# Elementwise work of the mixers moved from GpSimd to DVE and ScalarE in a hybrid decoder block

## The chip, the cores and the metric

The kernel runs on one core of a Trainium2 chip. TensorE (PE) multiplies matrices into PSUM; DVE (VectorE), ScalarE (ACT) and GpSimd (POOL) do elementwise work; SP and ACT issue the DMAs. Each engine takes its instructions strictly in the order written, and semaphores order them between engines. The metric is the device time of one execution in microseconds; before the change the median of three runs is 1366.57 us (1365.25 to 1368.38).

## The reference

One decoder layer on 1024 tokens of width 1024, float32. A normalised input is projected by one matrix; sixteen heads mix the tokens in three ways; an output projection and a squared-ReLU MLP follow.

```python
proj = rms_norm(x, norm1_g) @ w_in            # split into hq hf hi hg | sq sk sv | fq fk fv ff
# 4 HGRN heads (per head 64 keys, 64 values), in chunks of 64 tokens:
b = cumsum(log_f);  k = (1 - lb) * sigmoid(-f)
A[t,s] = sum_k q[t,k] k[s,k] exp(b[t,k] - b[s,k])          # s <= t, inside a chunk
o = (q * exp(b)) @ S + A @ v;  S = exp(b_end) * S + (k * exp(b_end - b)).T @ v
o_hg = rms_norm(o, hg_norm_g) * silu(hg)
# 6 stick-breaking heads, q and k RMS-normed per head, s < t:
z = q @ k.T / 8;  A = exp(log_sigmoid(z) + sum over later s of log_sigmoid(-z))
# 6 forgetting heads, q and k RMS-normed: softmax(q @ k.T / 8 + c_t - c_s), s <= t
x = x + concat(o_hg, A_sb @ sv, A_fox @ fv) @ w_out
x = x + square(relu(rms_norm(x, norm2_g) @ w_ff1)) @ w_ff2
```

## The kernel before

All large products run as three matmuls on split operands: each float32 matrix is cut into a rounded high part and the rest (`split`, L129: the high part by ScalarE or a chosen engine, the low part by a subtraction), and high x high, high x low and low x high are summed (`mm3`, L173 to L176).

The mixing stage works through eight units in the order of `CFG["ORDER"]`: m0, hg0, m1, m2, m3, hg1, m4, m5. A unit m*i* is a pair of one stick-breaking and one forgetting head ("pair i" below); a unit hg*j* is two HGRN heads. While the core of one unit runs, the projection of the next is computed: `tok` (L289) and `qf`/`ig` (L601, L612) are its matmuls (tile `pj`), `w_steps` (L204) loads its eight weight slices into four raw buffers and splits them (tiles `whi`, `wlo`; the letter of `CFG["LO"]` at the unit's place names the engine of the low part, V for DVE and G for GpSimd). `finish` (L307) squares keys and queries (`qsq`), sums the squares and scales the keys (`kraw`). During the last unit's core the output weights are split (`woh`, `wol`, L820) and the output projection starts (`po`).

The stick-breaking part (`qtile`, L404 to L418) clips the scores, takes exp and log on ScalarE, sums from the right by a DVE scan (`sbr`, L413), subtracts that sum from the scores (`sbz`, L416) and takes exp again. `qprep` (L360) copies and scales the queries on GpSimd (`qd`).

The HGRN core (`hgrn`, L629) replaces the decay inside a chunk by six levels of blocks, 32 down to 1 tokens wide. At each level and for each half of the tokens, DVE subtracts the value of `b` at the block's middle (`hx`, L671), ScalarE takes two exponentials (L673, L674), four products with the queries give `hxq` (L676, per half and head) and two with the keys update `hx` (L677); PE then multiplies (`hz`, L681) and DVE copies the result under a mask (`hat`, L692). The diagonal (`hqk`, L698), the state (`hkd`, L714 to L716, and `hb`, L725) and the output (L742 to L790) follow. The gates of a core, `hg_gates` (L568), are computed before it.

The order of instructions on each engine is not the order of this code. The builder runs its own timeline estimate over the program and places each instruction by it (`TCARGS`, L35), with the order of the timed steps (L906 to L923) and the priority of the weight splits (`HPW`) as its input. A change of engine at one line therefore moves instructions on all engines. Pools of fixed numbers of buffers (`CFG["BUFS"]`: five `zs` buffers hold `hx`, `hkd`, `sbz`) limit how far it can run ahead.

Of the kernel before, what the change touches and what calls it, by code (L numbers as in the profile page):

```python
# [12 lines left out]
AF = mybir.ActivationFunctionType  # L13
ALU = mybir.AluOpType
# [4 lines left out]
P = 128  # L19
# [4 lines left out]
HD = 64  # L24
# [31 lines left out]
    "GT": ["pair", "pair", "pair"],
# [9 lines left out]
def hybrid_block(ctx, tc, x, lb_logits, norm1_g, w_in, hg_norm_g, sb_q_g, sb_k_g, fox_q_g, fox_k_g,  # L66
# [215 lines left out]
    def proj_attn(name, pr):  # L282
# [24 lines left out]
        def finish(half):  # L307
            q8, k8 = (a.rearrange("p t a d -> p (t a) d") for a in (st["q"][half], st["kr"][half]))
            ss = small.tile([P, 16], F32, name="qss")
            for e, a in enumerate((k8, q8)):  # L310
                sq = big("dt", "qsq", [P, 8, HD])
                ENG[CFG["FE"][pr][0]].tensor_tensor(out=sq, in0=a, in1=a, op=ALU.mult)
# [3 lines left out]
            ENG[CFG["FE"][pr][1]].tensor_tensor(out=k8, in0=k8, in1=r[:, 0:8].unsqueeze(2).broadcast_to([P, 8, HD]), op=ALU.mult)

# [37 lines left out]
    def attn(name):  # L355
# [23 lines left out]
        def qtile(h, i):  # L379
# [16 lines left out]
            for c, w in reversed(pcs):  # L396
# [7 lines left out]
                if sbk:  # L404


                    e = big("e", "sbe")[:, :w]
                    zs = big("zs", "sbz")[:, :w]
                    V.tensor_scalar(out=zs, in0=z, scalar1=st["r"][i // 4][:, i % 4, 0:1], scalar2=ZMAX, op0=ALU.mult, op1=ALU.min)  # L409
                    S.activation(e, zs, AF.Exp)  # L410
                    S.activation(e, e, AF.Ln, bias=1.0)  # L411
                    r = big("r", "sbr")[:, :w]
                    V.tensor_tensor_scan(out=r[:, ::-1], data0=e[:, ::-1], data1=zero_t[:, 0:1].broadcast_to([P, w]),  # L413
                                         initial=0.0 if prev is None else prev, op0=ALU.add, op1=ALU.add)
                    prev = r[:, 0:1]
                    ENG[CFG["SUB"][pr]].tensor_tensor(out=zs, in0=zs, in1=r, op=ALU.subtract)  # L416
# [151 lines left out]
    def hg_gates(name, half):  # L568
# [60 lines left out]
    def hgrn(name):  # L629
# [16 lines left out]
        def level(n):  # L646
            def lv(t):
                return t.rearrange("p (b e n) -> p b e n", e=2, n=n)
# [17 lines left out]
            for half in range(2):  # L666
# [8 lines left out]
                for h in range(2):  # L675
                    ENG[CFG["HQ"][pr][h]].tensor_tensor(out=qv(xq, h, half), in0=qv(x_, h, None), in1=qv(q, h, None), op=ALU.mult)  # L676
                ENG[CFG["HK"][pr]].tensor_tensor(out=lv(x_)[:, :, 0, :], in0=lv(x_)[:, :, 0, :], in1=lv(k)[:, :, 0, :], op=ALU.mult)  # L677
            ph = pt("zt"[li % 2], "hz")
# [28 lines left out]
        def state():  # L707
            eb = small.tile([P, NC_], F32, name="heb")
            kt = []
            for half in range(2):  # L710
# [4 lines left out]
                S.activation(kd, kd, AF.Exp)  # L715
                G.tensor_tensor(out=kd, in0=kd, in1=k, op=ALU.mult)  # L716
                S.activation(eb[:, half * HC:(half + 1) * HC], bend.rearrange("p c o -> p (c o)"), AF.Exp)
# [6 lines left out]
                S.activation(b, b, AF.Exp)  # L724
                G.tensor_tensor(out=b, in0=b, in1=st["q"][half], op=ALU.mult)  # L725
            u = [pt("t", "hu") for _ in range(2)]
# [15 lines left out]
        def output():  # L742
# [9 lines left out]
            for h in range(2):  # L752
# [15 lines left out]
            for hf in range(2):  # L768
# [543 lines left out]
```

## Time and profile before

| | before |
|---|---|
| median of three runs | 1366.57 us (1365.25 to 1368.38) |
| the profiled execution | 1366.46 us, span 1364.7 us |
| mean granted PE clock | 0.975 |
| PE busy | 1290.6 us, 95% |
| DVE busy | 979.0 us, 72% |
| ACT busy | 715.6 us, 52% |
| POOL busy | 261.5 us, 19% |
| HBM read, written | 104.40 MB, 43.54 MB |

The page gives the busy time of each engine, the span in forty slices, the chain of work that ended last, and the costliest groups of instructions. A group's row reads: line, engine, operation, out<-in by the program's names, shapes and how many; then busy us in all and the mean ns of one; then the idle time just before them and what ended it. A row of the slices shows the slice, then busy time and instruction count of PE, of PE's weight loads (PEld), DVE, ACT and POOL, then the granted PE clock (1.00 is full), the DMA share and GB/s. A row of the timeline shows start, duration, engine, line and operation, how many instructions were merged, and in brackets the idle time before it and what ended it.

### The profile page before, as it was taken

What the parts mean: (1) busy time and instruction counts of PE and PEld (TensorE: products, weight loads), DVE (VectorE), ACT (ScalarE), POOL (GpSimd) and SP (SyncE); (2) the same over time, 40 slices, a digit from 0 to 9 for tenths busy, and PEclk for the clock granted to TensorE, in tenths of its full rate; (3) what the DMA queues carried; (4) which work ended last, traced back from release to release, by engine and by line L of the source; (5) the groups of instructions that cost most, each with busy time, mean ns of one, the idle gap of its engine ahead of it and who ended that gap; (6) DMA issues with size and microseconds to landing.
All of it is one profiled execution on the core that took longest, in us unless ns stands there. A gap on an engine that the chain in (4) does not pass through costs nothing.

```text
span 1364.7 us, 19810 instructions
## 1 busy us (share of the span) xinstructions
PE 1290.6 (95%) x7200; PEld 1066.1 (78%) x7200; DVE 979.0 (72%) x1712; ACT 715.6 (52%) x1537; POOL 261.5 (19%) x294
## 2 busy tenths in 40 slices
PE   4999989999999789799798999999999899999998
PEld 4978878878788688477586888888887788888887
DVE  6768677866576977975568766666656898786865
ACT  5557445878687336774445554545454533333430
POOL 7112693413125843420100000000000000000000
PEclk9999999999999989899898999999999999999999
DMA  8200220201102020333353444344435983634322
GB/s 217 56 17 19 60 42 22 63 24 45 34 16 63 9 55 24 122 118 109 124 161 125 131 163 141 129 162 162 138 121 189 373 289 98 200 119 142 121 78 93
DMA packets 125930, 149.24 MB, mean 109 GB/s; under 512 B 46460, under 2 KB 73084, under 8 KB 125832
## 3 DMA queue, kind: packets, MB, share of 16 engines
q1 hardware_dynamic: 100464, 101.79, 24.5%
q10 hardware_dynamic: 25368, 46.17, 9.6%
q8 instruction: 57, 0.93, 0.3%
q14 instruction: 41, 0.34, 0.1%
HBM read 104.40 MB, written 43.54 MB: 108 GB/s over the span
## 4 chain that ended last, share of the span: by engine, by line
PE 83%; DVE 7%; ACT 4%; POOL 2%; issue 2%; DMA 1%; SPq 0%; ACTq 0%; POOLq 0%; DVEq 0%
PE pj L174 7%; PE pj L176 6%; PE pj L175 6%; PE av L474 4%; PE atp L455 3%; PE pd L1201 2%; PE pc L1024 2%; PE pc L1023 2%; PE pc L1022 2%; PE pd L1022 2%; PE pd L1023 2%; PE pd L1024 2%; PE pc L1202 2%; PE pc L1203 2%; PE pc L1201 2%; PE pa L1022 2%
## 5 line engine op out<-in xcount | busy, mean ns | idle before, releaser
L174 PE MATMUL pj<-whi,hTh 128*128 128x384 f32 (+2 forms) x512 | 171.7, 338 | 1.8 <-DVE vst L303 1.8
L176 PE MATMUL pj<-whi,hTl 128*128 128x384 f32 (+2 forms) x512 | 171.9, 336 | 0.0
L175 PE MATMUL pj<-wlo,hTh 128*128 128x384 f32 (+2 forms) x512 | 171.6, 336 | 0.2 <-POOL wlo L134 0.2
L131 ACT CAST fah<-ya 128x1024 fp32r<-128x1024 f32 x56 | 58.7, 1048 | 166.2 <-PE pd L1202 50.0
L174 PEld LDWEIGHTS pj<-whi,hTh 128*128 128x128 f32 x512 | 98.6, 193 | 5.8 <-issue 3.1
L176 PEld LDWEIGHTS pj<-whi,hTl 128*128 128x128 f32 x512 | 98.5, 192 | 2.2 <-issue 1.7
L175 PEld LDWEIGHTS pj<-wlo,hTh 128*128 128x128 f32 x512 | 98.5, 193 | 2.1 <-POOL wlo L134 0.7
L134 DVE TENSOR_TENSOR fal<-ya,fah 128x1024 fp32r<-128x1024 f32 x56 | 68.2, 1218 | 21.5 <-ACT fah L131 21.3
L474 PE MATMUL av<-at,vst 128*64 128x256 f32 x480 | 71.7, 383 | 2.0 <-DVE at L461 0.9
L134 POOL TENSOR_TENSOR wlo<-wraw,whi 128x384 fp32r<-128x384 f32 (+2 forms) x56 | 60.7, 1111 | 32.8 <-ACT whi L131 16.1
L459 ACT COPY at<-atp 128x128 f32<-128x128 f32 (+3 forms) x120 | 55.3, 476 | 12.4 <-PE atp L455 12.2
L474 PEld LDWEIGHTS av<-at,vst 128*64 128x64 f32 x480 | 38.1, 143 | 28.7 <-issue 8.0
L400 PE MATMUL z<-kst,qj 128*128 128x512 f32 (+3 forms) x144 | 51.9, 388 | 8.2 <-ACT qj L375 4.6
L134 DVE TENSOR_TENSOR fbl<-w2raw,fbh 128x1024 fp32r<-128x1024 f32 x48 | 57.9, 1214 | 1.6 <-ACT fbh L131 1.6
L417 ACT ACTIVATE sbz<-sbz 128x128 f32<-128x128 f32 (+3 forms) x72 | 37.6, 526 | 40.6 <-DVE sbz L416 26.6
L174 PE MATMUL po<-woh,mTh 128*128 128x512 f32 x128 | 52.6, 411 | 2.5 <-DVE x L858 2.4
L409 DVE TENSOR_SCALAR sbz<-z,qnr 128x128 f32<-128x128 f32 (+3 forms) x72 | 42.6, 611 | 15.7 <-PE z L403 10.1
L131 ACT CAST fbh<-w2raw 128x1024 fp32r<-128x1024 f32 x48 | 50.0, 1048 | 6.5 <-DMA w2raw<-in_w_ff_dram 5.1
L413 DVE TENSOR_TENSOR_SCAN sbr<-sbe,zero_t 128x128 f32<-128x128 f32 (+3 forms) x48 | 42.5, 894 | 14.8 <-ACT sbe L411 11.9
L434 ACT ACTIVATE fxa<-fxa,fxmn 128x512 f32<-128x512 f32 (+2 forms) x72 | 43.8, 610 | 17.0 <-DVE fxmn L431 9.6
L401 PE MATMUL z<-kst,qj 128*128 128x512 f32 (+3 forms) x144 | 50.8, 379 | 1.3 <-DVE qj L376 1.2
L1201 PE MATMUL pd<-fbh,fah 128*128 128x512 f32 x128 | 49.6, 400 | 2.2 <-ACT fbh L131 2.2
(356 smaller groups left out, 3783.5 us busy)
## 6 DMA issues: line engine op xcount, KB each, us to landing
w1raw<-in_w_ff_dram SPq DMA_DIRECT2D x32, 512.0 KB, 5.5
w2raw<-in_w_ff_dram SPq DMA_DIRECT2D x16, 1024.0 KB, 6.6
ya<-yd_s SPq DMA_DIRECT2D x32, 512.0 KB, 3.8
yd_s<-y ACTq DMA_DIRECT2D x48, 256.0 KB, 4.6
ya<-yd_a SPq DMA_DIRECT2D x24, 512.0 KB, 4.0
wraw<-in_w_in_dram SPq DMA_DIRECT2D x48, 192.0 KB, 3.1
wraw<-in_w_in_dram SPq DMA_DIRECT2D x16, 256.0 KB, 4.3
xraw<-in_x_dram SPq DMA_DIRECT2D x16, 256.0 KB, 3.1
```

What stands on the lines that cost most here:

```text
L131: S.copy(hi, raw)
L134: lo_eng.tensor_tensor(out=lo, in0=raw, in1=hi, op=ALU.subtract)
L174: PE.matmul(o, lhsT=lh, rhs=rh, start=start, stop=False)
L175: PE.matmul(o, lhsT=lh, rhs=rl, start=False, stop=False)
L176: PE.matmul(o, lhsT=ll, rhs=rh, start=False, stop=stop)
L400: PE.matmul(z, lhsT=qj[:, 0, qs], rhs=kst[:, :w], start=True, stop=False)
L459: S.copy(dst, tv)
L474: PE.matmul(o[h * HD:(h + 1) * HD, c0:], lhsT=st["v"][j // 4][:, j % 4, h, :], rhs=at[h][j // 4][:, j % 4, c0:], start=(j == 0), stop=(j = ...
L1022: PE.matmul(o, lhsT=wh[:, k], rhs=bh[:, k], start=start and k == 0, stop=False, **kw)
L1023: PE.matmul(o, lhsT=wh[:, k], rhs=bl[:, k], start=False, stop=False, **kw)
L1024: PE.matmul(o, lhsT=wl[:, k], rhs=bh[:, k], start=False, stop=k == 3, **kw)
L1201: PE.matmul(o, lhsT=lh[:, ts], rhs=rh, start=start and q == q0, stop=False, **kw)
```

## The change

These operations leave GpSimd for DVE: the products of the HGRN levels that were still there (half of L676, all of L677), the HGRN gate's addition (L586), the products of the diagonal, of the state and of the output norm's gain (L698, L716, L725, L774), the scaling of the keys (L316, pairs 0, 1, 2 and 4), the stick-breaking subtraction of pairs 1 and 5 (L416), and the low part of the weight splits of pairs 1 and 4 (`LO`). The squares of keys and queries (L312; DVE had pair 3's) and of the HGRN output (L763) go to ScalarE as activations. GpSimd keeps the queries (`qd`), the memsets, the weight splits of pairs 0, 2 and 5 and of hg1, and the first half of the output weights. Four lines of `CFG` go, so lines of the changed kernel stand four lower from there on (L676 becomes L672).

```diff
-    "LO": "GVGGVGGG",
+    "LO": "GVVGVGVG",
...
-    "SUB": "VGVVVG",
...
-    "FE": ["GG", "GG", "GG", "VV", "GG", "GV"],
-    "HQ": ["VG", "GV"],
-    "HK": "GG",
...
-                ENG[CFG["FE"][pr][0]].tensor_tensor(out=sq, in0=a, in1=a, op=ALU.mult)
+                S.activation(sq, a, AF.Square)
...
-            ENG[CFG["FE"][pr][1]].tensor_tensor(out=k8, in0=k8, in1=r[:, 0:8].unsqueeze(2).broadcast_to([P, 8, HD]), op=ALU.mult)
+            V.tensor_tensor(out=k8, in0=k8, in1=r[:, 0:8].unsqueeze(2).broadcast_to([P, 8, HD]), op=ALU.mult)
...
-                    ENG[CFG["SUB"][pr]].tensor_tensor(out=zs, in0=zs, in1=r, op=ALU.subtract)
+                    V.tensor_tensor(out=zs, in0=zs, in1=r, op=ALU.subtract)
...
-        G.tensor_tensor(out=a1, in0=a1, in1=t1, op=ALU.add)
+        V.tensor_tensor(out=a1, in0=a1, in1=t1, op=ALU.add)
...
-                    ENG[CFG["HQ"][pr][h]].tensor_tensor(out=qv(xq, h, half), in0=qv(x_, h, None), in1=qv(q, h, None), op=ALU.mult)
-                ENG[CFG["HK"][pr]].tensor_tensor(out=lv(x_)[:, :, 0, :], in0=lv(x_)[:, :, 0, :], in1=lv(k)[:, :, 0, :], op=ALU.mult)
+                    V.tensor_tensor(out=qv(xq, h, half), in0=qv(x_, h, None), in1=qv(q, h, None), op=ALU.mult)
+                V.tensor_tensor(out=lv(x_)[:, :, 0, :], in0=lv(x_)[:, :, 0, :], in1=lv(k)[:, :, 0, :], op=ALU.mult)
...
-                G.tensor_tensor(out=kd, in0=kd, in1=k, op=ALU.mult)
+                V.tensor_tensor(out=kd, in0=kd, in1=k, op=ALU.mult)
...
-                G.tensor_tensor(out=b, in0=b, in1=st["q"][half], op=ALU.mult)
+                V.tensor_tensor(out=b, in0=b, in1=st["q"][half], op=ALU.mult)
...
-                G.tensor_tensor(out=sq, in0=oh, in1=oh, op=ALU.mult)
+                S.activation(sq, oh, AF.Square)
```

(L698 and L774 change in the same way as L716.)

How the order of instructions changes, at the places of which the prediction speaks. First GpSimd at the end of the second HGRN core, before: the last two levels' products, the state's products, then the weight splits of pair 5.

```order
L677 TENSOR_TENSOR hx<-hx,hf 128x256
L676 TENSOR_TENSOR hxq<-hx,hq 64x8x32
L677 TENSOR_TENSOR hx<-hx,hf 128x256
L676 TENSOR_TENSOR hxq<-hx,hq 64x8x32
L716 TENSOR_TENSOR hkd<-hkd,hf 128x512
L725 TENSOR_TENSOR hb<-hb,hq 128x512
L716 TENSOR_TENSOR hkd<-hkd,hf 128x512
L725 TENSOR_TENSOR hb<-hb,hq 128x512
L134 TENSOR_TENSOR wlo<-wraw,whi 128x384 x4
```

GpSimd in the same stretch, with the change:

```order
L584 MEMSET ht_5083 128x512
L585 MEMSET ht_5083 128x8
L366 COPY qd<-qraw 128x256
L650 MEMSET hxq 128x1024 x2
L363 TENSOR_TENSOR qd<-qraw,qnr 128x256
L130 TENSOR_TENSOR wlo<-wraw,whi 128x384 x8
```

Between the clearing of `hxq` and pair 5's eight splits GpSimd now has one query tile and nothing of the HGRN core.

DVE at the end of the same core, before:

```order
L676 TENSOR_TENSOR hxq<-hx,hq 64x8x32
L671 TENSOR_TENSOR hx<-hb 128x512 x2
L327 SCALAR_TENSOR_TENSOR kst_5476<-ktp,gk_fx,kst_5476 64x512
L692 COPY_PREDICATED hat<-lm_872,hz 128x128x4
L714 TENSOR_TENSOR hkd<-hb 128x512 x2
L676 TENSOR_TENSOR hxq<-hx,hq 64x8x32 x2
L692 COPY_PREDICATED hat<-lm_880,hz 128x256x2
```

And with the change:

```order
L667 TENSOR_TENSOR hx<-hb 128x512 x2
L710 TENSOR_TENSOR hkd<-hb 128x512
L323 SCALAR_TENSOR_TENSOR kst_5476<-ktp,gk_fx,kst_5476 64x512
L688 COPY_PREDICATED hat<-lm_872,hz 128x128x4
L710 TENSOR_TENSOR hkd<-hb 128x512
L673 TENSOR_TENSOR hx<-hx,hf 128x256
L672 TENSOR_TENSOR hxq<-hx,hq 64x8x32 x2
L673 TENSOR_TENSOR hx<-hx,hf 128x256
L672 TENSOR_TENSOR hxq<-hx,hq 64x8x32 x2
L712 TENSOR_TENSOR hkd<-hkd,hf 128x512
L688 COPY_PREDICATED hat<-lm_880,hz 128x256x2
L721 TENSOR_TENSOR hb<-hb,hq 128x512
```

All products of the last level now follow each other on DVE, and the state's products stand between the masked copies.

ScalarE there, before (`whi` is the high part of pair 5's weights):

```order
L673 ACTIVATE hx<-hx 128x256
L674 ACTIVATE hx<-hx 128x256
L715 ACTIVATE hkd<-hkd 128x512
L724 ACTIVATE hb<-hb 128x512
L715 ACTIVATE hkd<-hkd 128x512
L724 ACTIVATE hb<-hb 128x512
L301 COPY qraw<-pj 128x128
L302 COPY kraw<-pj 128x128
L131 CAST whi<-wraw 128x384 x4
```

And with the change:

```order
L127 CAST whi<-wraw 128x384 x2
L669 ACTIVATE hx<-hx 128x256
L670 ACTIVATE hx<-hx 128x256
L127 CAST whi<-wraw 128x384 x2
L669 ACTIVATE hx<-hx 128x256
L670 ACTIVATE hx<-hx 128x256
L711 ACTIVATE hkd<-hkd 128x512
```

The first four high parts now stand among the last level's exponentials instead of behind the state's.

More of the change, by code (lines that the diff above doesn't have):

```diff
@@ L51 @@
     "KEYS": [4, 5, 5, 5, 5, 4],
-    "FE": ["GG", "GG", "GG", "VV", "GG", "GV"],
-    "HQ": ["VG", "GV"],
-    "HK": "GG",
-    "GP": [(0, 2), (0, 4)],
+        "GP": [(0, 2), (0, 4)],
     "GT": ["pair", "pair", "pair"],
@@ L697, in diag @@
                 qk = big("r", "hqk")
-                G.tensor_tensor(out=qk, in0=st["q"][half], in1=st["f"][half], op=ALU.mult)
+                V.tensor_tensor(out=qk, in0=st["q"][half], in1=st["f"][half], op=ALU.mult)
                 for m in range(4):
@@ L773, in output @@
                 onf = on.rearrange("p m h v -> p (m h) v")
-                G.tensor_tensor(out=onf, in0=onf, in1=hgn.unsqueeze(1).broadcast_to([P, 8, HD]), op=ALU.mult)
+                V.tensor_tensor(out=onf, in0=onf, in1=hgn.unsqueeze(1).broadcast_to([P, 8, HD]), op=ALU.mult)
                 s_ = big("e", "hsg", [P, 4, 2, HD])
```

## The prediction

> **What bounds the kernel now.** First the page: busy shares, GpSimd's busy tenths in 40 slices of 34.1 us, and the chain of work that ended last.
>
> ```profile
> PE 1290.6 (95%) x7200; PEld 1066.1 (78%) x7200; DVE 979.0 (72%) x1712; ACT 715.6 (52%) x1537; POOL 261.5 (19%) x294
> POOL 7112693413125843420100000000000000000000
> PE 83%; DVE 7%; ACT 4%; POOL 2%; issue 2%; DMA 1%; SPq 0%; ACTq 0%; POOLq 0%; DVEq 0%
> ```
>
> TensorE sets the time; it idles 74 us of the span. So the change can win only where PE waits, or where its granted clock drops. GpSimd's tenths are 0 from the 21st slice on, so the change lies in the first 682 us, the mixing stage, which I read in slices of 20 us (each engine's busy time and instructions, then the granted PE clock).
>
> ```profile
> 100.00:120.00 20.00, 20.00 (x160) 18.25 (x160) 17.63 (x36) 15.38 (x39) 5.75 (x7) 1.00 0.04 15
> 120.00:140.00 20.00, 20.00 (x150) 17.33 (x149) 17.45 (x29) 12.46 (x30) 8.00 (x6) 1.00 0.20 40
> ...
> 160.00:180.00 20.00, 17.89 (x222) 15.68 (x218) 17.29 (x30) 6.58 (x20) 18.40 (x19) 0.99 0.04 14
> 180.00:200.00 20.00, 19.83 (x206) 17.89 (x204) 12.19 (x18) 8.41 (x20) 19.02 (x17) 0.93 0.20 41
> 200.00:220.00 20.00, 17.13 (x177) 14.03 (x176) 11.89 (x35) 9.05 (x28) 7.36 (x9) 0.83 0.20 41
> ...
> 260.00:280.00 20.00, 18.87 (x125) 15.20 (x123) 17.18 (x39) 18.93 (x44) 8.50 (x8) 1.00 0.22 59
> 280.00:300.00 20.00, 18.36 (x112) 14.94 (x113) 11.39 (x30) 15.11 (x41) 1.63 (x3) 0.91 0.06 22
> ...
> 440.00:460.00 20.00, 19.14 (x197) 16.66 (x195) 14.38 (x22) 5.00 (x17) 16.16 (x19) 1.00 0.04 14
> 460.00:480.00 20.00, 10.39 (x99) 9.59 (x99) 19.72 (x15) 8.13 (x20) 16.08 (x16) 0.82 0.03 6
> 480.00:500.00 20.00, 18.48 (x188) 17.24 (x192) 13.83 (x28) 4.06 (x11) 8.40 (x10) 0.75 0.35 87
> ...
> 540.00:560.00 20.00, 15.11 (x74) 9.55 (x72) 18.18 (x31) 11.73 (x31) 15.12 (x14) 0.83 0.26 81
> 560.00:580.00 20.00, 15.95 (x86) 11.00 (x86) 18.69 (x33) 15.93 (x37) 6.61 (x7) 0.91 0.47 141
> 580.00:600.00 20.00, 18.82 (x106) 12.95 (x107) 15.05 (x35) 18.17 (x46) 5.45 (x7) 0.91 0.32 109
> ```
>
> The gaps lie in four places, each with GpSimd at work. I count idle time, plus what the lowered clock took from busy time (1 minus clock, times busy): second HGRN core (440:500), 12.0 + 6.5 = 18.5 us; first HGRN core (160:220), 5.2 + 4.5 = 9.7; second attention pair (260:300), 2.8 + 1.7 = 4.5; output weights (540:600), 10.1 + 5.7 = 15.8. Together 48 us: the most that can be won there.
>
> The largest gap, in order of time, as DVE, GpSimd and PE each show it:
>
> ```profile
> 471.71 10.01 DVE L676 TENSOR_TENSOR hxq<-hx,hq 64x256 f32<-64x256 f32 x2
> ...
> 471.09 1.30 POOL L676 TENSOR_TENSOR hxq<-hx,hq 64x256 f32<-64x256 f32 x1
> 472.36 1.27 POOL L716 TENSOR_TENSOR hkd<-hkd,hf 128x512 f32<-128x512 f32 x1
> ...
> 476.04 1.25 POOL L725 TENSOR_TENSOR hb<-hb,hq 128x512 f32<-128x512 f32 x1
> 477.26 3.83 POOL L134 TENSOR_TENSOR wlo<-wraw,whi 128x384 fp32r<-128x384 f32 x4
> ...
> 481.52 0.77 PE L681 MATMUL hz<-hxq,hx 128*64 128x64 f32 x9 [8.48 <-DVE hxq L676]
> ```
>
> Two small DVE products take 10.01 us and end just after GpSimd's run of two-input operations. PE waits 8.48 us. The same product elsewhere:
>
> ```profile
> 168.22 0.42 DVE L676 TENSOR_TENSOR hxq<-hx,hq 64x256 f32<-64x256 f32 x1 [1.43 <-PE hz L681]
> 168.56 0.68 DVE L671 TENSOR_TENSOR hx<-hb 128x512 f32<-128x512 f32 x1
> ...
> 466.36 0.42 DVE L676 TENSOR_TENSOR hxq<-hx,hq 64x256 f32<-64x256 f32 x1
> 466.81 1.29 DVE L671 TENSOR_TENSOR hx<-hb 128x512 f32<-128x512 f32 x2
> ```
>
> 0.42 us when left alone, against a mean of 1.251 below: DVE and GpSimd hold each other up.
>
> [...]
>
> **The change part by part.** Groups by shape (busy us, mean ns):
>
> ```profile
> L676 DVE TENSOR_TENSOR hxq<-hx,hq 64x256 f32<-64x256 f32 x24 | 29.0, 1251 | 2.7 <-PE hz L681 2.6
> L416 DVE TENSOR_TENSOR sbz<-sbz,sbr 128x512 f32<-128x512 f32 x24 | 20.5, 852 | 0.2
> L671 DVE TENSOR_TENSOR hx<-hb 128x512 f32<-128x512 f32 x24 | 19.0, 826 | 0.5 <-PE atp L455 0.4
> L316 DVE TENSOR_TENSOR kraw<-kraw,qnr 128x512 f32<-128x512 f32 x4 | 2.8, 689 | 0.1
> ...
> L677 POOL TENSOR_TENSOR hx<-hx,hf 128x256 f32<-128x256 f32 x24 | 23.8, 1001 | 19.0 <-ACT hx L673 18.4
> L676 POOL TENSOR_TENSOR hxq<-hx,hq 64x256 f32<-64x256 f32 x24 | 22.8, 960 | 1.1 <-PE hz L681 0.4
> L312 POOL TENSOR_TENSOR qsq<-qraw 128x512 f32<-128x512 f32 x10 | 11.5, 1150 | 0.0
> ...
> L155 ACT ACTIVATE n1sq<-x_t 128x512 f32<-128x512 f32 x16 | 10.0, 627 | 2.8 <-DMA x_t<-in_x_dram 2.8
> L70 ACT ACT_TABLE_LOAD x1 | 1.3, 1283 | 0.8 <-PEq L1299 0.8
> ```
>
> DVE gains 48 HGRN products (24 of L676, 24 of L677) at 0.42 = 20.2 us; 20 operations of 128x512 (L586, L698, L716, L725, L774, four each) and 8 key scalings at 0.69 = 19.3; 24 subtractions (12 of 512 columns at 0.69, 12 narrower at some 0.45) = 13.7; 16 weight splits of 384 columns (pairs 1 and 4) at 0.55, between the two = 8.8. Pair 3's four squares leave it: 4 x 0.69 = 2.8. Sum +59 us. Against that its own two-input operations get shorter: 24 x (1.251 - 0.42) = 19.9, 24 x (0.852 - 0.689) = 3.9 and 24 x (0.826 - 0.645) = 4.3, together 28. Query scaling, half the weight splits and the output weights keep GpSimd reading, so I take 22. Net +37: DVE goes from 979 to some 1016 us, 75% of the span. The ends are 0 on the path (it fits in DVE's idle time) and +37 (all of it ends in PE waits). Only 100:140 is near full, with 35.1 of 40 us; there pair 1's splits and the gates' additions add 8 x 0.55 + 2 x 0.69 = 5.8, 0.9 more than is free. I take **+3 us** for new waits, near the row.
>
> Squares on ACT: 24 + 4 at 0.627 = 17.6 us. They follow the copies of the same keys and queries on ACT itself, so a hop between engines goes. Square already runs among Exp and Ln with one table load, so I add none. ACT is 65% or less busy in the HGRN slices, which hides this at nothing. At 260:280 (18.93 of 20) and 580:600 (18.17) cover is thin: two squares each would cost at most 2.5. I take **+1**.
>
> The second core's 8.48 us gap goes, since L676, L716 and L725 no longer lie on GpSimd. What stays is L134's weight splits of pair 5: the order puts ScalarE's halves before the last exponentials, so four splits (3.83 us) can still hold up DVE's last products, with a clock dip behind. Of 18.5 I take 13: **-13**.
>
> In the first core the chain of waits runs over GpSimd:
>
> ```profile
> 187.87 1.27 POOL hb L725
> 189.14 1.23 POOL hkd L716
> 190.37 1.23 POOL hb L725
> 191.60 4.92 POOL wlo L134 x4
> ...
> 196.54 4.19 DMA wraw<-in_w_in_dram
> ```
>
> 8.65 us of GpSimd stands ahead of the next weight load, which needs the four raw buffers back. L716 and L725 leave that queue, so the splits of pair 2 start as soon as ScalarE's halves are there, and the load is issued some 4 to 8 us sooner. The 2.9 us idle and the 0.83 clock at 200:220 follow this load. Of 9.7 I take **-6**.
>
> Second pair: subtractions leave GpSimd, ACT stays full: **-2** of 4.5. Output weights: their sixteen splits' casts and subtractions stay on GpSimd; only two squares (2 x 1.15) leave from between them: **-3** of 15.8.
>
> Moving the second half's products has a price of its own: in the first core DVE wrote partitions 0 to 63 and the next operation started 0.34 us after (168.22 to 168.56); in the second it wrote 64 to 127 and the next started 0.45 after (466.36 to 466.81). Now the halves alternate, which is at most 48 changes of half, 5.3 us on DVE; it lies within the +3.
>
> [...]
>
> Sum: -13 - 6 - 2 - 3 + 3 + 1 = **-20 us**. The profiled execution took 1366.46 us (span 1364.7), the median is 1366.57: the forecast is **1346 us**. All gaps gone gives 1366.5 - 48 = 1318; no gap gone and all DVE work on the path gives 1366.5 + 37 = 1403.
>
> **The rivals.** *All four gaps close* (0.08): 1318 to 1330. For it: GpSimd works in each. Against: at 560:600 DVE or ACT is above 90% busy with little of GpSimd.
>
> *The gap is not GpSimd's* (0.12): if exclusion lasts one instruction only, at most 1.37 us, the 8.48 us has another cause and stays with the clock loss behind it; then -20 + 11 = -9, 1357. Against: DVE is shown busy, not waiting, for 10.01 us. [...]
>
> *The stall changes its engine* (0.12): each core gives DVE 24 x 0.42 + 10 x 0.69 = 17 us more; 440:500 has 12.1 free. If contention stays too (query scaling and pair 5's splits still read), 5 us overflow in the second core, 5 more come back as clock loss, and half of today's 12.0 idle with them: 16 of its 18.5 us. The first core keeps its loss, the +4 is paid, and 2 are won elsewhere: -2.5 + 4 - 2, no change, 1366.
>
> *Slower* (0.18): the HGRN levels become paced by DVE alone. Each level is two subtractions, exponentials on ACT, then six products in order on one engine; PE's in-order queue has the next group of products behind it. If PE waits 1 us at each of the six levels of both cores, that is 12 us idle, and the granted clock stays at 0.75, as at 480:500, through both cores: a quarter of their 48.0 + 54.9 us of busy time, 25.7. Together 37.7 against today's 28.2 there, and the +4: +13.5, or 1380. It decides once waits recur at every level. For it: DVE is busy 17.29 of 20 us at 160:180. Against: products now take 0.42 for 0.96 to 1.25.
>
> **How the numbers follow.** Forecast as summed 0.50, its own range 1336 to 1355; with the two faster rivals 0.70 faster. A measurement here tells 0.2% (2.7 us) from no change: 0.12 within it, 0.18 slower. The range for 8 in 10 is 1328 to 1375: from near the full gain to well into the slower case.
>
> **What would show it.** Right: L672 (was L676) on DVE at 0.42 to 0.6 mean; PE idle in the second core's 60 us below 5 us; no clock under 0.9 there; DVE busy at 1000 to 1025; ACT near 733; one table load. Wrong: PE waits of 1 us or more for DVE at each level, or DVE products still above 0.9 beside pair 5's splits; the output-weight gap grown; idle at 100:140, where PE now has none.

## The result, and the profile after

The changed kernel takes 1349.63 us (median of four, 1348.58 to 1352.5) against 1365.92 us of the kernel before on the same chip (1365.25 to 1368.38): ratio 0.9881, 95% interval 0.986 to 0.9902, or 16 us less. The forecast was 1346 us. The profiled execution took 1350.42 us, its span is 1348.4 us, the mean granted clock 0.983 for 0.975.

The page after: busy shares, GpSimd's tenths in 40 slices of 33.7 us, and the chain by engine.

```profile
PE 1283.8 (95%) x7200; PEld 1061.8 (79%) x7200; DVE 984.3 (73%) x1824; ACT 728.9 (54%) x1565; POOL 108.5 (8%) x154
POOL 7000020011210114200000000000000000000000
PE 82%; DVE 9%; ACT 5%; DMA 2%; issue 2%; SPq 0%; ACTq 0%; DVEq 0%
```

GpSimd loses 153 us of work, but DVE gains only 5 and ScalarE 13; GpSimd is gone from the chain. The slices of 20 us that answer to those of before (the output weights are split some 16 us earlier, 522.10 for 538.50, and stand in 520:580 here):

```profile
140.00:160.00 20.00, 17.75 (x101) 16.00 (x101) 13.50 (x37) 10.41 (x30) 0.40 (x1) 1.00 0.30 67
160.00:180.00 20.00, 20.00 (x196) 18.21 (x195) 14.84 (x36) 8.30 (x24) 2.89 (x3) 1.00 0.04 14
180.00:200.00 20.00, 16.12 (x173) 14.07 (x172) 19.62 (x32) 10.35 (x26) 8.89 (x8) 0.93 0.40 81
200.00:220.00 20.00, 18.57 (x257) 16.74 (x256) 13.26 (x35) 5.80 (x14) 0.40 (x1) 0.90 0.01 2
...
260.00:280.00 20.00, 17.27 (x114) 12.11 (x110) 16.82 (x40) 17.20 (x41) 1.84 (x3) 1.00 0.05 17
280.00:300.00 20.00, 18.29 (x104) 15.14 (x106) 12.86 (x38) 17.45 (x47) 2.19 (x4) 0.83 0.08 27
...
440.00:460.00 20.00, 20.00 (x195) 18.18 (x194) 15.72 (x35) 8.70 (x27) 2.42 (x3) 1.00 0.04 15
460.00:480.00 20.00, 18.02 (x176) 15.83 (x175) 19.60 (x33) 10.30 (x25) 9.11 (x8) 0.84 0.31 73
480.00:500.00 20.00, 20.00 (x268) 18.21 (x267) 13.99 (x37) 6.79 (x16) 1.01 (x2) 0.90 0.08 22
...
520.00:540.00 20.00, 18.21 (x104) 13.73 (x103) 16.90 (x32) 15.28 (x40) 14.38 (x15) 0.91 0.32 97
540.00:560.00 20.00, 15.13 (x73) 9.44 (x71) 18.84 (x36) 16.61 (x40) 4.94 (x5) 1.00 0.42 141
560.00:580.00 20.00, 16.88 (x105) 11.90 (x104) 16.81 (x43) 18.96 (x44) 2.69 (x4) 1.00 0.24 80
```

Counted as in the prediction (idle time, plus busy time multiplied by 1 minus the clock): the second HGRN core (440:500) loses 2.0 + 4.9 = 6.9 us where it lost 18.5; the first (160:220) 5.3 + 3.0 = 8.3 for 9.7, but the slice ahead of it, 140:160, now idles 2.25 for 0.6; the second attention pair (260:300) 4.4 + 3.1 = 7.5 for 4.5; the output weights 9.8 + 1.6 = 11.4 for 15.8.

Where the largest gap was, in order of time:

```profile
473.73 1.10 PE L677 MATMUL hz<-hxq,hx 128*64 128x64 f32 x16 [1.04 <-DVE hxq L672]
474.05 1.56 DVE L672 TENSOR_TENSOR hxq<-hx,hq 64x256 f32<-64x256 f32 x2
474.29 1.03 POOL L130 TENSOR_TENSOR wlo<-wraw,whi 128x384 fp32r<-128x384 f32 x1 [2.27 <-ACT whi L127]
475.64 0.69 DVE L712 TENSOR_TENSOR hkd<-hkd,hf 128x512 f32<-128x512 f32 x1
```

The pair of products that took 10.01 us takes 1.56: one of the two (1.13 us) still waits beside a split on GpSimd, for that one instruction. PE waits 1.04 us for 8.48. DVE's groups after:

```profile
L672 DVE TENSOR_TENSOR hxq<-hx,hq 64x256 f32<-64x256 f32 x48 | 24.3, 505 | 5.7 <-POOL hxq L650 3.8 <-PE hz L677 1.4
L412 DVE TENSOR_TENSOR sbz<-sbz,sbr 128x512 f32<-128x512 f32 x36 | 26.1, 725 | 0.4
L667 DVE TENSOR_TENSOR hx<-hb 128x512 f32<-128x512 f32 x24 | 16.6, 717 | 6.2 <-PE atp L451 6.1
L409 DVE TENSOR_TENSOR_SCAN sbr<-sbe,sbr,zero_t 128x512 f32<-128x512 f32 x24 | 31.7, 1321 | 1.0 <-ACT sbe L407 0.9
L130 DVE TENSOR_TENSOR wlo<-wraw,whi 128x384 fp32r<-128x384 f32 x24 | 12.7, 549 | 2.2 <-ACT whi L127 2.2
```

48 products now take less in all (24.3 us) than 24 did (29.0). This group of scans had 1533 ns before; another of the same width, 12 without a carried-in sum, grew from 1275 to 1383.

To compare kernels whose stages begin at other times, the rest uses one measure: PE's lost time (idle time, plus busy time multiplied by 1 minus the granted clock) between landmarks of the program, summed from all PE and clock records of each profiled execution. An HGRN core runs from its first level's matmul (`hz`) to its last output matmul, the last mixing stage from there to the last transpose of the second norm (`n2tp`). The end of PE's last matmul minus the loss lies between 1260 and 1266 us in all fourteen kernels, so the loss tells nearly all of their differences.

| us lost | until first core | first core | pairs m1 to m3 | second core | m4, m5, output | MLP | all |
|---|---|---|---|---|---|---|---|
| before | 19.3 | 8.7 | 8.2 | 18.0 | 29.3 | 14.9 | 98.4 |
| after | 20.5 | 8.7 | 7.9 | 7.1 | 23.6 | 13.5 | 81.3 |

The loss falls by 17.1 us, 10.9 of it in the second core and 5.7 in the last mixing stage. The first core shows no gain.

How far such a row can be trusted: each is one execution. Kernels that write the same instructions in the same order up to some place give repeats of the stages ahead of it. The changed kernel and `e11` below are the same for their first 522 us, and so are `e1` and `e12`; their rows differ by 0.1 and 2.7 us until the first core, 0.6 and 0.5 in it, 1.4 and 4.9 in m1 to m3, 1.1 and 0.1 in the second core. The kernel before and `e9` are the same up to 227 us and differ by 1.6 us in each of the first two columns; the changed kernel and `e8`, the same up to 302 us, by 1.9 and 0.7. So a difference of 2 us in a core, or of 5 in m1 to m3, is not told from chance; the last two stages have no such repeat.

### The profile page after: what moved, and what is told of

The parts are those of the page before. It is cut to its first block, busy times and chain, and to the rows that moved or that the text cites. A ratio compares the mean times of both kernels' runs of the same rounds, so it can differ in the third digit from the quotient of the medians.

```text
span 1348.4 us, 19713 instructions
## 1 busy us (share of the span) xinstructions
PE 1283.8 (95%) x7200; PEld 1061.8 (79%) x7200; DVE 984.3 (73%) x1824; ACT 728.9 (54%) x1565; POOL 108.5 (8%) x154
## 4 chain that ended last, share of the span: by engine, by line
PE 82%; DVE 9%; ACT 5%; DMA 2%; issue 2%; SPq 0%; ACTq 0%; DVEq 0%
PE pj L170 7%; PE pj L172 6%; PE pj L171 6%; PE av L470 4%; PE atp L451 2%; PE pc L1019 2%; PE pc L1020 2%; PE pc L1018 2%; PE pd L1018 2%; PE pd L1019 2%; PE pd L1020 2%; PE pc L1198 2%; PE pc L1199 2%; PE pc L1197 2%; PE pa L1020 2%; PE pa L1018 2%
## 5 line engine op out<-in xcount | busy, mean ns | idle before, releaser
L170 PEld LDWEIGHTS pj<-whi,hTh 128*128 128x128 f32 x512 | 98.4, 192 | 3.9 <-issue 1.3
L455 ACT COPY at<-atp 128x128 f32<-128x128 f32 (+3 forms) x120 | 55.9, 478 | 15.8 <-PE atp L451 15.6
L470 PEld LDWEIGHTS av<-at,vst 128*64 128x64 f32 x480 | 37.8, 141 | 27.9 <-issue 6.9
L405 DVE TENSOR_SCALAR sbz<-z,qnr 128x128 f32<-128x128 f32 (+3 forms) x72 | 42.7, 612 | 19.0 <-PE z L399 10.5
L409 DVE TENSOR_TENSOR_SCAN sbr<-sbe,zero_t 128x128 f32<-128x128 f32 (+3 forms) x48 | 42.0, 879 | 14.6 <-ACT sbe L407 13.4
L1198 PE MATMUL pa<-fbl,fah 128*128 128x512 f32 x128 | 50.3, 397 | 1.9 <-DVE fbl L130 1.9
L171 PE MATMUL po<-wol,mTh 128*128 128x512 f32 x128 | 51.7, 404 | 0.0
L1197 PE MATMUL pa<-fbh,fah 128*128 128x512 f32 x128 | 49.1, 395 | 1.9 <-ACT fbh L127 1.9
```

The costliest lines, as they stand in the source:

```text
L170: PE.matmul(o, lhsT=lh, rhs=rh, start=start, stop=False)
L171: PE.matmul(o, lhsT=lh, rhs=rl, start=False, stop=False)
L455: S.copy(dst, tv)
L470: PE.matmul(o[h * HD:(h + 1) * HD, c0:], lhsT=st["v"][j // 4][:, j % 4, h, :], rhs=at[h][j // 4][:, j % 4, c0:], start=(j == 0), stop=(j = ...
L1197: PE.matmul(o, lhsT=lh[:, ts], rhs=rh, start=start and q == q0, stop=False, **kw)
L1198: PE.matmul(o, lhsT=lh[:, ts], rhs=rl, start=False, stop=False, **kw)
```

## The experiments

Theory A: GpSimd's instructions that read SBUF hold up DVE's two-input instructions, and through them the `hz` matmuls; taking the HGRN products off GpSimd wins the second core. Rivals: the attention part or the splits did it; or the gain is one of order, since every edit makes the builder write all engines' streams anew. All ratios are against the kernel before, run beside it on the same chip; the chips differ, so ratios are compared and not medians.

### The three parts alone

`e1_hgrn_only`: the kernel before, with the HGRN products, the gates' addition, the output norm's gain and its square moved as in the change.

```diff
-    "HQ": ["VG", "GV"],
-    "HK": "GG",
+    "HQ": ["VV", "VV"],
+    "HK": "VV",
...
-                G.tensor_tensor(out=kd, in0=kd, in1=k, op=ALU.mult)
+                V.tensor_tensor(out=kd, in0=kd, in1=k, op=ALU.mult)
```

> The kernel before, with only the HGRN part of the change (levels, gate addition, diagonal, state, output gain to DVE, output squares to ScalarE). Theory A (DVE and GpSimd block each other on two-input operations): the DVE products of the levels fall from a mean of 1.25 us to under 0.6, the 8.48 us wait of PE in the second core goes, and most of the gain is here: 9 to 13 us less than before, 1353 to 1357. Theory B (the gain is the new order as a whole, or the attention part): under 4 us less, 1362 or more.

`e2_attention_only`: only the keys' and queries' squares (to ScalarE), the scaling of the keys and the stick-breaking subtraction (to DVE).

```diff
-    "SUB": "VGVVVG",
+    "SUB": "VVVVVV",
-    "FE": ["GG", "GG", "GG", "VV", "GG", "GV"],
+    "FE": ["GV", "GV", "GV", "VV", "GV", "GV"],
...
-                ENG[CFG["FE"][pr][0]].tensor_tensor(out=sq, in0=a, in1=a, op=ALU.mult)
+                S.activation(sq, a, AF.Square)
```

> The kernel before, with only the attention part (squares of keys and queries to ScalarE, key scaling and stick-breaking subtraction to DVE). Theory A: the HGRN products stay blocked (mean over 1 us on DVE), a PE wait of some 8 us stays in the second core, and the time falls by 2 to 6 us from what leaves GpSimd beside the output weights: 1360 to 1364. Theory B: half or more of the 16 us comes from here, 1358 or less.

`e3_splits_only`: only the low parts of the weight splits of pairs 1 and 4 to DVE.

```diff
-    "LO": "GVGGVGGG",
+    "LO": "GVVGVGVG",
```

> The kernel before, with only the low parts of the weight splits of pairs 1 and 4 on DVE. Theory A: nothing that PE waits for is blocked by these splits, so within 3 us of before (1363 to 1369). Theory B (order alone moves the time): a change of more than 3 us either way.

| | median us | ratio (95%) | first core | m1 to m3 | second core | m4, m5, output | all lost |
|---|---|---|---|---|---|---|---|
| e1, HGRN | 1353.84 | 0.9896 (0.9865 to 0.9928) | 2.7 | 8.8 | 7.5 | 30.0 | 83.5 |
| e2, attention | 1360.95 | 0.9948 (0.993 to 0.9967) | 12.5 | 8.2 | 14.0 | 25.4 | 92.3 |
| e3, splits | 1379.2 | 1.0086 (1.0055 to 1.0117) | 10.0 | 13.4 | 19.0 | 32.4 | 113.9 |

The HGRN part alone comes out as theory A has it, with 10.5 us less lost in the second core; the whole gain, some 14 us by the ratio, is above the 9 to 13 expected, and 6.0 of it lie in the first core. With the splits alone the old stall stands there unchanged, eight GpSimd instructions long. The timeline of e3:

```profile
483.38 10.04 DVE L676 TENSOR_TENSOR hxq<-hx,hq 64x256 f32<-64x256 f32 x2
484.04 1.28 POOL L716 TENSOR_TENSOR hkd<-hkd,hf 128x512 f32<-128x512 f32 x1
...
488.96 3.84 POOL L134 TENSOR_TENSOR wlo<-wraw,whi 128x384 fp32r<-128x384 f32 x4
...
493.22 1.98 PE L681 MATMUL hz<-hxq,hx 128*64 128x64 f32 x32 [7.58 <-DVE hxq L676]
```

e2 missed in part: the stall was to stay at 8 us, and its longest wait is 3.4; its gain, some 7 us by the ratio, is above the 2 to 6 expected. The expectation of e3 missed: it is slower by 0.9%, more than 3 us, as theory B has it. Its losses are larger in every stage, but in the two cores only by 1.3 and 1.0 us, which is within chance. Sixteen more splits on DVE or the new order can be the reason; this run doesn't part them.

### The parts together

`e5_without_splits`: the HGRN and attention parts, with `LO` as before. `e10_hgrn_and_splits`: the HGRN part and the splits, attention as before. (The change is all three; the edits are shown against the changed kernel, whose `CFG` has no `SUB` and `FE`. The scaling of the keys changes in the same way.)

```diff
-    "LO": "GVVGVGVG",
+    "LO": "GVGGVGGG",
```

> The changed kernel without its move of the splits of pairs 1 and 4 (these stay on GpSimd; HGRN and attention parts as changed). If parts add (14.2 and 7.1 us less in the two single runs, 11.8 more with the splits alone): ratio to before 0.983 to 0.987, below the changed kernel's 0.988, and the first attention pair's products end some 5 us earlier (no PE wait for a split on DVE near 146 us). Rival (what the splits cost is an accident of the order in that one kernel): ratio 0.988 or more.

```diff
+    "SUB": "VGVVVG",
+    "FE": ["GG", "GG", "GG", "VV", "GG", "GV"],
...
-                S.activation(sq, a, AF.Square)
+                ENG[CFG["FE"][pr][0]].tensor_tensor(out=sq, in0=a, in1=a, op=ALU.mult)
...
-                    V.tensor_tensor(out=zs, in0=zs, in1=r, op=ALU.subtract)
+                    ENG[CFG["SUB"][pr]].tensor_tensor(out=zs, in0=zs, in1=r, op=ALU.subtract)
```

> The kernel before with the HGRN part and the splits of pairs 1 and 4, without the attention part. With the HGRN part alone at 0.9896, all three at 0.9881, and HGRN with attention at 0.9944: if the parts add, 0.997 to 1.000 (HGRN 14 less, splits 12 more); if what the splits and the attention part cost depends on the order they fall into, and only the HGRN core's gain is fixed, anything from 0.984 to 0.998, with the second core at 44 to 47 us in every case.

| | median us | ratio (95%) | first core | m1 to m3 | second core | m4, m5, output | all lost |
|---|---|---|---|---|---|---|---|
| e5 | 1362.02 | 0.9944 (0.9929 to 0.996) | 8.1 | 19.0 | 6.6 | 26.8 | 93.6 |
| e10 | 1362.19 | 0.9936 (0.9912 to 0.9961) | 7.6 | 10.6 | 8.6 | 29.3 | 93.3 |
| after | 1349.63 | 0.9881 (0.986 to 0.9902) | 8.7 | 7.9 | 7.1 | 23.6 | 81.3 |

The parts don't add. Attention alone won 0.5%; on top of the HGRN part it costs 0.5% (0.9896 to 0.9944). Splits alone lose 0.9%; on top of HGRN and attention they win 0.6%. e5's expectation, which added, missed by 10 us or more, and its ratio lies where the rival has it, by which what the splits cost is an accident of the order; the table has 11.1 more than after in m1 to m3 (19.0), above the 4.9 that the repeats differ by. e10 lies in the second of its expected ranges, the one for parts that don't add, and its second core is 46.9 us long, inside the 44 to 47. What does repeat is the second core: adding the HGRN part takes it from 18.0 to 7.5 (before to e1), from 14.0 to 6.6 (e2 to e5) and from 19.0 to 8.6 (e3 to e10).

### The same work in another order

`e8_shifted_after` and `e9_shifted_before`: the changed kernel and the kernel before, each with the planned start times of four units moved by 0.01 or 0.02. No operation changes its engine.

```diff
-    "SPAN": [(0, 0), (0, -0.1), (0, 0), (-0.1, 0.05), (-0.1, 0), (-0.1, 0), (0.15, 0), (-0.05, 0)],
+    "SPAN": [(0, 0), (0, -0.1), (0.02, 0), (-0.12, 0.05), (-0.1, 0), (-0.12, 0), (0.15, 0), (-0.06, 0)],
```

> The changed kernel with the start times of four units' cores moved by 0.01 to 0.02 of a unit, which changes some 600 rows of PE's order and no engine's work. It tells how much the order alone moves the time: theory A expects the second HGRN core (45.8 us) within 2 us and the whole within 5 us of the changed kernel (ratio to before 0.984 to 0.992). If the gain of the change is luck of one order, the ratio goes to 0.995 or more.

> The kernel before with the same four start times moved as in the shifted changed kernel (some 860 rows of PE's order, no engine's work). Theory A (the second HGRN core is held up by GpSimd whatever the order): that core stays 52 us or longer (54.9 before), and the whole change measured under this second order, shifted changed against this, is 8 to 20 us. If the gain is luck of one order, this kernel comes within 5 us of the shifted changed one (ratio to before 0.994 or less).

| | median us | ratio (95%) | first core | m1 to m3 | second core | m4, m5, output | all lost |
|---|---|---|---|---|---|---|---|
| e9, before | 1365.79 | 0.9965 (0.9949 to 0.998) | 10.3 | 15.8 | 8.9 | 22.1 | 93.7 |
| e8, after | 1354.11 | 0.9889 (0.9861 to 0.9917) | 8.0 | 12.1 | 2.1 | 28.4 | 87.1 |

Order alone makes the old work 0.35% faster; in these executions m1 to m3 lose 7.6 us more and the last stage 7.2 less. Under this order the whole change gives 0.9889 / 0.9965 = 0.9924 (0.989 to 0.996, the two intervals combined as squares): some 10 us, not 16, inside the 8 to 20 that theory A expected. e8's ratio is that of the changed kernel, as expected; its second core, 43.2 us, is 2.6 shorter than the changed kernel's 45.8, where 2 were allowed. The second core gains under both orders, 10.9 and 6.8 us; the last stage does not (-5.7 and +6.3), and m1 to m3 (-0.3 and -3.7) stay within chance. e9 missed its expected length of that core (52 us or more): it is 50.6, against 54.9 before and 43.2 in e8, since its worst wait there is 5.4 us. There two subtractions (`hx`, L671; mean of the 24 is 0.954 us, 0.717 after) take 4.99 us beside GpSimd's reads, and no product is held for more than 1.75. So how long DVE is held, and which instruction, is a matter of order; that it is held is not.

### Reads or mere presence of GpSimd

`e6_gpsimd_reads` puts GpSimd work back that nothing waits for: at each level and half, right behind `hx` L677, a subtraction of a spare tile from itself (24 of 128x512). `e7_gpsimd_writes` puts two fills (MEMSET) there instead, 2 x 526 ns for the subtraction's 1117. A copy of one column of `hx` ties both to that place.

```diff
+                G.tensor_copy(pad[:, 0:1], x_[:, 0:1])
+                G.tensor_tensor(out=pad, in0=pad, in1=pad, op=ALU.subtract)
```

> The changed kernel with, per level and half, one GpSimd subtraction of a 128x512 scratch tile from itself behind a one-column copy of hx (24 extra subtractions in all; nothing waits for their result but the next one). Theory A (GpSimd reading SBUF blocks two-input DVE work): DVE's level products rise from a mean of 0.505 to 0.75 us or more and the HGRN cores (first level to last output product, 46.4 and 45.8 us) get 3 us or more longer each. Rival B (time follows what PE waits for, not GpSimd): products stay under 0.6, cores within 2 us.

```diff
+                G.tensor_copy(pad[:, 0:1], x_[:, 0:1])
+                G.memset(pad, 0.0)
+                G.memset(pad, 0.0)
```

> The same with two GpSimd memsets of the scratch tile in place of each subtraction (48 extra memsets, about as long in GpSimd time, which write and do not read). Theory A: DVE's level products stay under 0.6 us and the cores within 2 us of the changed kernel's. Rival B (any GpSimd work at that place costs): the same as with the subtractions.

The groups of e6:

```profile
L676 DVE TENSOR_TENSOR hxq<-hx,hq 64x256 f32<-64x256 f32 x48 | 27.6, 574 | 7.2 <-POOL hxq L654 6.0 <-PE hz L683 0.7
L679 POOL TENSOR_TENSOR pad<-pad 128x512 f32<-128x512 f32 x24 | 26.8, 1117 | 1.6
L677 DVE TENSOR_TENSOR hx<-hx,hf 128x256 f32<-128x256 f32 x24 | 15.0, 623 | 1.2 <-ACT hx L673 0.5
```

Two rows of its timeline, in the second core:

```profile
466.97 1.22 POOL L679 TENSOR_TENSOR pad<-pad 128x512 f32<-128x512 f32 x1
467.33 1.15 DVE L677 TENSOR_TENSOR hx<-hx,hf 128x256 f32<-128x256 f32 x1
```

The same groups of e7, with one of its two fills:

```profile
L676 DVE TENSOR_TENSOR hxq<-hx,hq 64x256 f32<-64x256 f32 x48 | 24.5, 510 | 8.5 <-POOL hxq L654 7.4 <-PE hz L684 0.6
L677 DVE TENSOR_TENSOR hx<-hx,hf 128x256 f32<-128x256 f32 x24 | 11.0, 456 | 1.2 <-ACT hx L673 0.6
L680 POOL MEMSET pad<- 128x512 f32 x24 | 12.6, 526 | 1.2
```

And its timeline at the same product:

```profile
465.85 0.53 POOL L679 MEMSET pad<- 128x512 f32 x1
466.39 0.42 DVE L677 TENSOR_TENSOR hx<-hx,hf 128x256 f32<-128x256 f32 x1
466.44 0.53 POOL L680 MEMSET pad<- 128x512 f32 x1
```

| | median us | ratio (95%) | first core | m1 to m3 | second core | m4, m5, output | all lost |
|---|---|---|---|---|---|---|---|
| e6, reads | 1366.44 | 0.9974 (0.9958 to 0.9991) | 14.6 | 14.1 | 7.9 | 27.9 | 100.0 |
| e7, writes | 1357.85 | 0.9912 (0.9881 to 0.9943) | 11.3 | 13.0 | 4.2 | 29.7 | 91.5 |

Beside a subtraction of 1.22 us the product takes 1.15; between two fills it takes 0.42, as when alone. Reads cost 8.6 us more than writes, 7.0 of them in the two cores (3.3 and 3.7), though the two kernels' orders differ too. The mean of the products was expected at 0.75 or more with reads: it is 0.574, since 24 separate reads hold a product for one instruction at most, 1.25 us being the longest, and 37 of the 48 take less than 0.6. The cores, expected 3 us or more longer each, are 4.9 and 2.9 longer with reads; with writes, where 2 were allowed, 2.5 longer and 0.6 shorter. So it is GpSimd's reading that lengthens these products (means of 0.574 and 0.623 us with reads, 0.510 and 0.456 with writes), not its being busy. Holds of one instruction are shown here; the row of eight was only taken away (e1, e5, e10) or left (e3), never put back.

### What is left on GpSimd

`e4_all_splits_dve`: the changed kernel, with the splits of pairs 2 and 5 on DVE as well. `e11_output_weights`: the changed kernel, with the first half of the output weights split on ScalarE and DVE.

```diff
-    "LO": "GVVGVGVG",
+    "LO": "GVVVVGVV",
```

> The changed kernel, with the splits of pairs 2 and 5 on DVE too, so that GpSimd reads nothing but query tiles during the HGRN cores. Theory A: the level products fall from a mean of 0.505 to 0.45 us or less, the PE waits of 2.4 and 1.1 us in the first core and 1.0 and 0.6 in the second go with their clock dips, 3 to 7 us less than the changed kernel: 1343 to 1347. Rival (DVE is full there, 19.6 of 20 us in both cores' worst slice): 16 more splits at 0.55 us cost 2 to 5 us, 1352 to 1355.

```diff
-    "WX": ["GG", "AV"],
+    "WX": ["AV", "AV"],
```

> The changed kernel with the first half of the output weights split on ScalarE and DVE in place of GpSimd (8 casts of 0.62, 8 subtractions of 0.69 us). If GpSimd's reads are what holds up the 520:580 stretch (9.8 us idle there): 3 to 6 us less than the changed kernel, ratio to before 0.983 to 0.986. If DVE and ScalarE are full there (52.6 and 50.8 of 60 us): 5 us or more slower than the changed kernel, ratio 0.991 or more.

`e12_hgrn_and_output`: the kernel before with the HGRN part (the edit of e1) and the edit of e11, nothing else.

> The kernel before with two edits only: the HGRN moves, and the output-weight splits taken from GpSimd (casts on ACT, subtractions on DVE). The attention products, squares and pair splits stay where they were before. Theory A (GpSimd's reads of SBUF hold up DVE in the two places, and the two places are far enough apart to add): 0.9896 for the HGRN part alone, less the 0.003 that the output weights won on the whole change, so 0.983 to 0.990; second HGRN core 43 to 47 us. Rival (a new order of the instruction streams costs or gives some 7 us at places that the edit does not touch): 0.991 to 0.995, with the second core still at 43 to 47 us.

| | median us | ratio (95%) | first core | m1 to m3 | second core | m4, m5, output | all lost |
|---|---|---|---|---|---|---|---|
| e4 | 1362.38 | 0.9946 (0.9927 to 0.9966) | 6.8 | 15.2 | 1.6 | 33.7 | 94.1 |
| e11 | 1349.6 | 0.9852 (0.9829 to 0.9875) | 8.1 | 9.3 | 6.0 | 24.9 | 82.8 |
| e12 | 1353.81 | 0.988 (0.984 to 0.9921) | 3.2 | 13.7 | 7.6 | 22.3 | 86.3 |

The group of products in e4:

```profile
L672 DVE TENSOR_TENSOR hxq<-hx,hq 64x256 f32<-64x256 f32 x48 | 20.1, 419 | 10.0 <-POOL hxq L650 7.7 <-PE hz L677 1.8
```

Its slice 540:560:

```profile
540.00:560.00 20.00, 15.29 (x51) 10.78 (x52) 17.08 (x34) 14.17 (x34) 7.15 (x8) 0.66 0.43 132
```

With no split left on GpSimd beside the levels, every product takes the 0.42 us it takes alone (mean 0.419, longest 0.458), and the second core loses 1.6 us, the least of all kernels (e8 comes to 2.1 with these splits still on GpSimd). But m1 to m3 and the last stage lose 17.4 us more than after, with the clock at 0.66 in the slice shown: the kernel is slower than the changed one by 0.65% in ratio, some 9 us, where theory A expected 3 to 7 us less and its rival 2 to 5 us more, so both missed. Cleaning up the contended place isn't enough where other places lose more, by the new order or by the 16 splits that DVE gains.

e11 has the lowest ratio and lies in its expected interval, but its place doesn't show the reason. The slices of e11 at the output weights:

```profile
520.00:540.00 20.00, 17.28 (x95) 13.46 (x95) 18.40 (x43) 19.32 (x49) 1.35 (x2) 0.91 0.46 145
540.00:560.00 20.00, 17.34 (x103) 11.69 (x100) 18.08 (x38) 18.82 (x43) 0.61 (x1) 1.00 0.30 102
560.00:580.00 20.00, 17.57 (x83) 12.29 (x83) 14.87 (x39) 17.87 (x43) 1.95 (x3) 0.83 0.29 97
```

GpSimd is nearly gone (3.9 us for 22.0 after), yet they lose 7.8 + 4.5 = 12.3 us, against 11.4 after. Its median and span (1349.6, 1347.9) are those of the changed kernel (1349.63, 1348.4), its lower ratio comes with a kernel before that took 1371.17 us on that chip, and the two ratios' intervals overlap: the two aren't told apart. e12 lies where theory A has it, but its interval reaches into the rival's, and it isn't told apart from the HGRN part alone (0.9896). No kernel here clearly beats the changed one.

## Why the prediction was right, and where it was wrong

The time was right (1346 for 1349.63, 3.6 us low, inside 1336 to 1355). By its steps:

- **The second core, -13: right, -11.6** by the prediction's slices, -10.9 by landmarks. That pair 5's splits would still hold up the last products with a clock dip behind is what the rows at 473.73 to 475.64 show, and the clock of 0.84. Of its signs, PE's idle time (2.0 us, below 5) and the products' mean (0.505, inside 0.42 to 0.6) came; "no clock under 0.9" failed, and one sign of being wrong showed in part: two single products beside pair 5's splits take 1.15 and 1.13 us, above its 0.9. The rival that the gap is not GpSimd's is out: e1 closes it, e3 leaves it, e6 and e7 tell reads from writes.
- **The first core, -6: wrong, next to nothing came** (8.7 and 8.7 by landmarks; 9.7 and 8.3 by slices, with 1.7 more idle in the slice ahead of them). The step "the splits of pair 2 start as soon as ScalarE's halves are there, and the load is issued some 4 to 8 us sooner" held, and by more: the eight issues of the load run from 26.1 to 36.2 us into the core before, and from 9.8 to 24.4 after. With the repeats (10.3 in e9; 8.0 and 8.1 in e8 and e11) the core gains 1.2 us in the mean. What failed is that 6 us hang on the load. First, PE's idle time behind the levels hardly changes, 1.6 us before and 1.4 after. Before:

```profile
193.64 10.05 SPq L219 DMA_DIRECT2D wraw<-in_w_in_dram  x8
...
202.40 0.33 PE L750 MATMUL hz<-hsa,hb 64*64 64x64 f32 x4 [1.13 <-DVE hsa L738]
```

  After:

```profile
211.19 0.33 PE L746 MATMUL hz<-hsa,hb 64*64 64x64 f32 x4 [0.85 <-DVE hsa L734]
```

  PE waits for the same sums of the state (`hsa`) in both. The chain that ended last runs to them over the load, ScalarE's halves and the queries before; after, it runs over the copies of the keys (`kst`), and no load is in it. Second, the splits now fall into the levels. Before, they ran behind the last level; after, they hold DVE in the middle of the levels: with the clock counted, the levels lose 4.8 us for 3.8 (4.5 in both repeats for 3.8), and the part behind them 3.9 for 4.9 (3.5 and 3.6 for 6.5).

```profile
181.60 4.42 POOL L130 TENSOR_TENSOR wlo<-wraw,whi 128x384 fp32r<-128x384 f32 x4 [12.41 <-ACT whi L127]
...
182.64 14.52 SPq L215 DMA_DIRECT2D wraw<-in_w_in_dram  x8
182.81 2.35 DVE L672 TENSOR_TENSOR hxq<-hx,hq 64x256 f32<-64x256 f32 x2
...
185.31 0.69 PE L677 MATMUL hz<-hxq,hx 128*64 128x64 f32 x16 [2.36 <-DVE hxq L672]
```

  The two products take 2.35 us beside four splits in a row, and PE waits 2.36 us. In e1 the splits come late, 22.6 us into the core, and the 6 us are won: 8.7 to 2.7 lost, no half clock at all in the core, which is 5.0 of the 6.0. Its timeline:

```profile
189.87 7.63 POOL L134 TENSOR_TENSOR wlo<-wraw,whi 128x384 fp32r<-128x384 f32 x6 [7.27 <-ACT whi L131]
```

  PE's waits for the products in that core (total, times, longest):

```profile
PE hz L681 <- DVE hxq L676: 1.3, 1, 1.3
```

  e12 has the same places and 3.2 lost; e5 and e10, with the splits 13.3 and 18.5 us into the core, wait up to 1.7 and 2.0 us at once and lose 8.1 and 7.6. That the splits' place decides fits these five kernels; it wasn't moved alone.
- **The second pair, -2: wrong, +3** in its slices. GpSimd's share there fell from 10.1 to 4.0 us of 40 and the loss rose, so less work on GpSimd did not bring a gain. Over the whole of m1 to m3 it is -0.3, within chance, and under the second order the old work went from 8.2 to 15.8 there.
- **The output weights, -3: -4.4 came**, but e11 takes GpSimd's splits away and wins nothing at that place, and under the second order the old work lost 7.2 us less in this stage (29.3 to 22.1 in e9). The number was met, the reason ("only two squares leave from between them") is not shown.
- **DVE's load, +37: mis-sized, +5.3** (979.0 to 984.3; 1000 to 1025 was named). The relief was taken as 22 us; the same 59 added give 54. The prediction listed products and subtractions, and left out that other instructions are relieved too: the four groups of scans of 512, 384 and 256 columns fell from 74.6 to 68.3 us in all, and two groups with one tensor input (TENSOR_SCALAR, `qnv` and `hf`) from 9.9 to 4.1. The rest is not itemised here. (The 0.645 us of its third term stands in no row; the median of these subtractions is 0.685, which makes the term 3.4 for 4.3.) So neither rival on DVE's load had its condition, the stall that changes its engine and the slower one: no wait recurs at each level, and 100:140, where the prediction feared an overflow, runs without PE idle.
- **ScalarE's squares, +1, and one table load: right** as far as the page shows (728.9 us busy, 733 named). The "+3" of new waits can't be read apart from the order; the price of the change of half neither: a free pair of products takes 0.84 us, twice 0.42, and nothing on PE's path shows it.

The sum was right partly because two errors met: -6 and -2 did not come, and about as much came from the last stage and the MLP (-5.7 and -1.4), where the prediction had only -3. To that extent it is luck that the sum met the time to 3.6 us. Under the other order the change is worth some 10 us, with 6.8 less lost in the second core in its two profiled executions. What stays open: what makes m1 to m3 lose from 7.9 to 19.0 us and the last stage from 22.1 to 33.7 in kernels of nearly the same work, and how much of that is the order and how much the single execution (up to 4.9 us in m1 to m3).

## What to carry to other kernels

Look for a short DVE instruction that takes many times its usual duration, and read which GpSimd instructions stand beside it: here a product of 0.42 us took 9.67 beside an unbroken row of eight that read SBUF (472.36 to 481.09), and moving that work to DVE won it; fills did no harm to these products (mean 0.510 us in e7, 0.505 after). A weight load or split that is let go sooner is no gain in itself (in the first core the load's issues began 16.3 us sooner, and 8.7 us were lost before and after): ask what runs beside its new place. And where a planner writes the order, test an edit under a second order, profile an unchanged stage more than once, and believe the part that both orders show at the same place.

## What the runs showed of the hardware that was not expected

- **A held DVE instruction can wait out a whole row of GpSimd instructions, but need not.** In the kernel before a product of 0.42 us was held through eight GpSimd instructions in a row, 472.36 to 481.09, and so it was in e3 (longest single product 9.671 and 9.696 us). Another product before, from 460.07, took 2.43 us and spans two whole instructions; the longest in e2 took 3.02. With the HGRN work gone from GpSimd, the longest product takes 1.23 us in the changed kernel, 1.23 to 1.27 in e1, e5, e6, e7, e10 and e11, and 0.46 in e4. In the changed kernel, beside the four splits from 181.60, which have no idle time between them, the two products took 1.21 and 1.12 us, one after each split. What decides between the two is not shown.
- **An instruction with one tensor input is held too.** In e9 a TENSOR_SCALAR whose mean is 0.18 us after (`qnv`, 12 of them, 0.43 before) took 3.17, through two GpSimd instructions:

```profile
475.13 3.17 DVE L142 TENSOR_SCALAR qnv<-qss 128x16 f32<-128x16 f32 x1
475.77 1.26 POOL L716 TENSOR_TENSOR hkd<-hkd,hf 128x512 f32<-128x512 f32 x1
477.00 1.27 POOL L725 TENSOR_TENSOR hb<-hb,hq 128x512 f32<-128x512 f32 x1
```

- **Half-clock periods can follow small waits.** Apart from the one in each kernel that the span's end cuts off, the periods at a granted clock of 0.50 are 3.4, 6.8, 10.2 or 13.7 us long in the kernels before and after, multiples of 3.4, and they do not need a long gap: in the changed kernel the one at 473.8 us (10.2 us long) follows 1.85 us of PE's idle time, in pieces, within the 3.4 us ahead of it; the others there follow 0.7 to 2.9. The amount alone does not decide: in the same kernel PE's wait of 2.36 us that ends at 185.31 stands ahead of full clock, which lasts until 197.3. Within the span 45.2 us ran at half clock, 69.2 before: the 24.0 us between them are worth 12.0 us of full-clock work.
